# Both products of each MLP as one level of Strassen's scheme, with h kept in memory as seven summed operands

## The chip, the cores and the metric

One core of one Trainium2 chip. The metric is the device time of one execution in microseconds, median over runs. Engines: TensorE (PE, its weight loads shown apart as PEld), VectorE (DVE), ScalarE (ACT), GpSimd (POOL) and SyncE (SP), whose queue issues most DMAs here.

## The reference

A decoder trunk of two layers on x of 1024 tokens by D = 1024, in float32. Layer 0 mixes with an S5 state-space block, layer 1 with stick-breaking attention, whose K and V are projected from the output of layer 0. After each mixer comes an MLP with 4096 hidden features, and each is closed by a layer norm over a scaled residual:

```python
mix = s5_mixer(...)                 # layer 0;  stick_breaking_attention(...) in layer 1
x = layer_norm(DEEPNORM_ALPHA * x + mix, ln_mix_g[layer], ln_mix_b[layer])
h = jnp.square(jax.nn.relu(x @ mlp_w1[layer] + b1))     # 1024 x 4096
ff = h @ mlp_w2[layer] + b2                             # 1024 x 1024
x = layer_norm(DEEPNORM_ALPHA * x + ff, ln_mlp_g[layer], ln_mlp_b[layer])
```

## The kernel before

Every product runs as three matmuls on split operands: a tensor is cast to fp32r by ScalarE (`hi`) and the remainder is formed by VectorE (`lo`), in `split`; a product is hi·hi + hi·lo + lo·hi. Raw weights come by SP in blocks of 128x512 (256 KB, `load_w`).

After its mixer a layer runs `proj_ln`: the output projection by token tile t = 0..7, then per tile the residual, `layer_norm`, and the transposes of y into the activation operand of the MLP (x1T in layer 0, x3T in layer 1). `layer_norm` of one tile goes bn_stats on VectorE, a power on GpSimd, a shift on ScalarE, a scaling on VectorE and the addition of b on GpSimd.

`mlp` has 32 blocks f of 128 hidden features. For each, `up` makes 48 matmuls of 128x128 by 128x512 into two PSUM banks (m0ph, m1ph), `up_act` applies Relu and Square on ScalarE and splits h on VectorE; h stays on chip. `down` takes chunks of two f blocks (the last has four), and for each of the 8 token tiles makes matmuls into m0py or m1py, which VectorE adds into the tile y (m0/m1 are the layers). In the first chunk GpSimd adds the bias b2 to y, in the last every token tile ends in its layer norm and store, or, in layer 0, in the transposes for the K and V projections. `VProject` follows layer 0's MLP. The up of the next chunk is issued between two downs. For the first four f blocks the first token half runs before the transposes of tokens 4 to 7. Pools of weight tiles give the distance by which loads run ahead; instructions within an engine are executed in the order in which they stand.

The lines that matter: L107 `split`'s subtraction, L106 its cast, L154 to L166 the norm, L755 to L759 the down matmuls, L92 to L96 the up matmuls, L764/L766 the additions into y, L768 the bias.

## Time and profile before

| | |
|---|---|
| median of 3 runs | 2547.64 us (2545.24 to 2548.4) |
| profiled execution, its own time | 2546.39 us |
| its span | 2544.7 us |
| TensorE busy | 2431.7 us, 96% |
| VectorE, ScalarE, GpSimd busy | 1503.3 (59%), 869.8 (34%), 537.0 us (21%) |
| DMA, mean | 76 GB/s |

The span is that of the records on the core; the time beside it includes what lies around. The page divides the span in 40 slices of 63.6 us. The MLPs are the two long stretches of slices with digit 9 in TensorE and single digits of DMA.

### The profile page before, as it was taken

The page shows a single profiled execution, that of the slowest core. Times are in us where ns is not written, and L with a number is a line of the kernel's source. Part 1 is how long each engine was busy: PE and PEld are TensorE (multiplying, and loading weights), DVE is VectorE, ACT ScalarE, POOL GpSimd, SP SyncE. Part 2 cuts the span into 40 slices and gives each one's busy share as a digit, 9 for nine tenths or more (in the row PEclk, how much of TensorE's full clock was granted, in tenths as well). Part 3 has the DMA queues.
Part 4 walks back from the last instruction along what each step waited for, and adds up shares of the span by engine and source line. Part 5 has one row for each costly group of instructions (what it writes and reads, how often), then busy time and mean ns, then how long its engine had stood idle before and what let it go on. Part 6 is the DMA issues. An engine that isn't in the chain of part 4 may idle for free.

```text
span 2544.7 us, 31280 instructions
## 1 busy us (share of the span) xinstructions
PE 2431.7 (96%) x11712; PEld 2000.4 (79%) x11712; DVE 1503.3 (59%) x2364; ACT 869.8 (34%) x1707; POOL 537.0 (21%) x620
## 2 busy tenths in 40 slices
...
PEclk9989999999999999999999999998999999999999
...
DMA packets 126248, 194.07 MB, mean 76 GB/s; under 512 B 13968, under 2 KB 56976, under 8 KB 126096
## 3 DMA queue, kind: packets, MB, share of 16 engines
...
## 4 chain that ended last, share of the span: by engine, by line
PE 73%; DVE 8%; issue 3%; POOL 2%; DMA 1%; ACT 1%; POOLq 0%; SPq 0%; DVEq 0%; ACTq 0%
PE m0py L755 5%; PE m0py L757 5%; PE m0py L759 5%; PE m1ph L96 4%; PE m1ph L94 4%; PE m1ph L92 4%; PE m0ph L92 4%; PE m0ph L94 4%; PE m0ph L96 4%; PE m1py L755 4%; PE m1py L757 4%; PE m1py L759 4%; DVE qq L1001 2%; PE po L1028 2%; DVE be L1002 2%
## 5 line engine op out<-in xcount | busy, mean ns | idle before, releaser
L106 ACT CAST w_m<-r_m 128x512 fp32r<-128x512 f32 x256 | 151.6, 620 | 622.8 <-PE m1py L759 257.3
L161 POOL TENSOR_TENSOR rsm<-vem,nhalf 128x1 f32<-128x1 f32 x16 | 9.1, 571 | 1209.5 <-DVE vem L159 1209.5
L107 DVE TENSOR_TENSOR w_m<-r_m,w_m 128x512 fp32r<-128x512 f32 x256 | 195.1, 776 | 110.9 <-ACT w_m L106 110.5
L766 DVE TENSOR_TENSOR y<-y,m1py 128x512 f32<-128x512 f32 x224 | 144.7, 682 | 97.2 <-PE m1py L759 97.2
L766 DVE TENSOR_TENSOR y<-y,m0py 128x512 f32<-128x512 f32 x224 | 144.8, 683 | 96.0 <-PE m0py L759 95.8
L1001 DVE TENSOR_TENSOR_SCAN qq<-qq 128x128 f32<-128x128 f32 (+7 forms) x128 | 174.2, 1363 | 12.0 <-POOL qq L995 11.7
L96 PE MATMUL m1ph<-x3T_h,w_m 128*128 128x512 f32 x512 | 165.1, 394 | 0.0
L94 PE MATMUL m1ph<-x3T_l,w_m 128*128 128x512 f32 x512 | 165.1, 394 | 0.0
L92 PE MATMUL m1ph<-x3T_h,w_m 128*128 128x512 f32 x512 | 164.8, 394 | 0.0
L94 PE MATMUL m0ph<-x1T_l,w_m 128*128 128x512 f32 x512 | 163.9, 391 | 0.0
L96 PE MATMUL m0ph<-x1T_h,w_m 128*128 128x512 f32 x512 | 163.8, 391 | 0.0
L92 PE MATMUL m0ph<-x1T_h,w_m 128*128 128x512 f32 x512 | 163.6, 391 | 0.0
L755 PE MATMUL m0py<-w_m,m0hh 128*128 128x512 f32 x512 | 160.8, 393 | 0.7 <-DVE x1T_l L107 0.5
L755 PE MATMUL m1py<-w_m,m1hh 128*128 128x512 f32 x512 | 160.4, 392 | 0.7 <-DVE x3T_l L107 0.5
L757 PE MATMUL m1py<-w_m,m1hh 128*128 128x512 f32 x512 | 159.8, 392 | 0.0
L759 PE MATMUL m1py<-w_m,m1hl 128*128 128x512 f32 x512 | 159.7, 392 | 0.0
L759 PE MATMUL m0py<-w_m,m0hl 128*128 128x512 f32 x512 | 159.7, 392 | 0.0
L757 PE MATMUL m0py<-w_m,m0hh 128*128 128x512 f32 x512 | 159.6, 392 | 0.0
L729 DVE CAST m1hh<-m1hr 128x512 fp32r<-128x512 f32 x64 | 27.1, 423 | 207.3 <-ACT m1hr L728 207.3
L729 DVE CAST m0hh<-m0hr 128x512 fp32r<-128x512 f32 x64 | 27.1, 423 | 201.9 <-ACT m0hr L728 201.9
L1014 PE MATMUL pt<-ident,be 128*128 128x128 f32 x576 | 90.5, 281 | 33.3 <-DVE wTl L107 23.3
L106 ACT CAST wTh<-pt 128x512 fp32r<-128x512 f32 (+1 forms) x192 | 88.1, 486 | 85.4 <-PE pt L1014 84.8
...
## 6 DMA issues: line engine op xcount, KB each, us to landing
r_m<-in_w SPq DMA_DIRECT2D x256, 256.0 KB, 2.7
v_d<-vt POOLq DMA_DIRECT2D x16, 512.0 KB, 3.5
v<-v_d POOLq DMA_DIRECT2D x16, 512.0 KB, 5.1
khs<-kh POOLq DMA_DIRECT2D x32, 256.0 KB, 3.0
kls<-kl POOLq DMA_DIRECT2D x32, 256.0 KB, 2.9
o_d<-ob SPq DMA_DIRECT2D x128, 64.0 KB, 2.5
ol<-o_d SPq DMA_DIRECT2D x32, 256.0 KB, 3.3
r_win<-in_w_in SPq DMA_DIRECT2D x16, 256.0 KB, 3.4
```

The costliest lines, as they stand in the source:

```text
L92: pe.matmul(ps[h], wh, xa[0][:, k, half(h)], start=(k == 0), stop=False)
L94: pe.matmul(ps[h], wh, xa[1][:, k, half(h)], start=False, stop=False)
L96: pe.matmul(ps[h], wl, xa[0][:, k, half(h)], start=False, stop=(k == KD - 1))
L106: act.copy(hi, src)
L107: dve.tensor_sub(lo, src, hi)
L729: dve.tensor_copy(hh[:, half(h)], r)
L755: pe.matmul(ps[n], hh[:, tok(t)], wh[:, half(n)], start=a0, stop=False)
L757: pe.matmul(ps[n], hh[:, tok(t)], wl[:, half(n)], start=False, stop=False)
L759: pe.matmul(ps[n], hl[:, tok(t)], wh[:, half(n)], start=False, stop=a1)
L766: dve.tensor_add(ys, ys, ps[n])
L1001: dve.tensor_tensor_scan(out=rev, data0=rev, data1=rev, initial=1.0, op0=ALU.mult, op1=ALU.bypass)
L1014: pe.transpose(pt[:, b_], self.be[:, tok(s0 + b_)], ident)
```

## The change

The features, the hidden blocks and the tokens are each taken in halves (2 x 2 blocks), and the eight half products of each matrix product become seven, M1 to M7, of sums of blocks. In `proj_ln` the transposed y of tokens 0 to 3 gives operands B11 and B21, tokens 4 to 7 with `second` and `rest` the other five (B22 and T1 to T4). `mlp_up` goes through 16 pairs p of f blocks with the seven products in the order PROD, 12 matmuls each; the weight operands of four products are sums of w1 blocks made on VectorE. Products are combined into the four blocks of h, Relu and Square are applied, and the sums s1 to s4 and the blocks that the second product needs, seven tensors of 128x512 per pair, are stored to memory (h_d) out of GpSimd's queue. `mlp_down` loads them again: chunks of CH = 4 pairs, per product and pair one unit of 12 matmuls, whose h and w2 operands are prepared three units ahead (`LA`; in up the weight operands are made two products ahead), the sums of w2 on GpSimd. y is stored by `layer_norm` (xm0_d, xm1_d) and loaded again for `mlp_down`. The steps of up run over all 16 pairs, then down begins. The last two M4 units of the last chunk are ordered by token tile, with the norms of tokens 4 to 7 between. The function names of the MLP change from m0/m1 to m0/m1 for up and d0/d1 for down. The core of the diff:

```diff
+    class XOps:
...
+        def first(self, psp, tag, y, t):
+            for kq, (n_, r) in enumerate((("B11", self.r11), ("B21", self.r21))):
+                pt = transpose(psp, tag, y, kq, f"{self.nm}_{t}{kq}")
+                h_, l_ = [v[:, :, tok(t)] for v in self.op[n_]]
+                act.copy(h_, pt)
+                act.copy(r[:, :, tok(t)], pt)
+                dve.tensor_sub(l_, pt, h_)
+        def more(self, tp_, tag, rp):
+            for n_ in ("T1", "T2", "T3", "T4"):
+                self.op[n_] = self.two(tp_, tag, n_)
+            self.r12, self.r22 = [rp.tile([P, 4, HF], F32, name=f"{self.nm}r{i}2") for i in (1, 2)]
+        def second(self, psp, tag, y, t):
+            c = tok(t - 4)
+            pt = transpose(psp, tag, y, 0, f"{self.nm}_{t}0")
+            r = self.r11[:, :, c]
+            dve.tensor_sub(r, r, pt)
+            act.copy(self.r12[:, :, c], pt)
+            pt = transpose(psp, tag, y, 1, f"{self.nm}_{t}1")
+            act.copy(self.r22[:, :, c], pt)
+            h_, l_ = [v[:, :, c] for v in self.op["T1"]]
+            act.copy(h_, r)
+            dve.tensor_sub(l_, r, h_)
+        def rest(self):
+            def both(n_, r):
+                for k2 in range(2):
+                    k = slice(2 * k2, 2 * k2 + 2)
+                    h_, l_ = [v[:, k] for v in self.op[n_]]
+                    act.copy(h_, r[:, k])
+                    dve.tensor_sub(l_, r[:, k], h_)
+            pool.tensor_add(self.r11, self.r11, self.r22)
+            both("B22", self.r22)
+            both("T2", self.r11)
+            dve.tensor_sub(self.r12, self.r22, self.r12)
+            pool.tensor_sub(self.r21, self.r11, self.r21)
+            both("T3", self.r12)
+            both("T4", self.r21)
...
-            for ts in (range(4), range(4, 8)):
+            for ts in (range(4), range(4, 8)) if n == 0 else (range(4), (4, 5), (6, 7)):
...
+    PROD = ("M1", "M5", "M6", "M3", "M7", "M2", "M4")
+    XOP = {"M1": "B11", "M5": "T1", "M6": "T2", "M3": "B22", "M7": "T3", "M2": "B21", "M4": "T4"}
...
+    def mlp_up(l, xo, y_tiles, w1, nm, ypool, tpool, tag, side, uside):
...
+        def prod(p, m, w):
+            ps_, (xh, xl) = bank(p, m), xo.op[XOP[m]]
+            first = m in ("M1", "M5", "M2")
+            for k, (wh, wl) in enumerate(by_k([w])):
+                pe.matmul(ps_, wh, xh[:, k], start=first and k == 0, stop=False, skip_group_check=True)
+                pe.matmul(ps_, wh, xl[:, k], start=False, stop=False, skip_group_check=True)
+                pe.matmul(ps_, wl, xh[:, k], start=False, stop=k == 3, skip_group_check=True)
+        xs = ExitStack()
+        xo.more(tpool, tag, mkpool(xs, f"{nm}r", 1, side=side))
+        for i, (p, m) in enumerate(((0, "M1"), (0, "M2"), (1, "M1"), (1, "M2"))):
+            prod(p, m, w1[i])
+            xo.second(pst, "t", y_tiles[4 + i], 4 + i)
+        xo.rest()
...
+        def operand(p, m):
+            r = lambda i, j: raw[p, i - 1, j - 1]
+            if m in ("M1", "M2", "M4"):
+                src = {"M1": r(1, 1), "M2": r(1, 2), "M4": r(2, 2)}[m]
+            else:
+                src = raws[-1].tile([P, HF], F32, tag="raw", name=f"{nm}s{m}{p}")
+                if m == "M5":
+                    dve.tensor_add(src, r(2, 1), r(2, 2))
+                elif m == "M6":
+                    dve.scalar_tensor_tensor(src, sums[p, "M5"], -1.0, r(1, 1), op0=ALU.mult, op1=ALU.subtract)
+                elif m == "M3":
+                    dve.tensor_sub(src, r(1, 2), sums[p, "M6"])
+                else:
+                    dve.tensor_add(src, r(1, 1), r(2, 1))
+                sums[p, m] = src
+            t = sl[count[0] % len(sl)].tile([P, 2, HF], F32R, tag="w", name=f"w_{nm}1{m}{p}")
+            count[0] += 1
+            split(t[:, 0], t[:, 1], src)
+            return t[:, 0], t[:, 1]
...
+        def after(p, m):
+            if m in ("M1", "M5", "M6"):
+                keep(p, m)
+            elif m == "M3":
+                dve.tensor_add(h_new(p, "A21"), tmp[p, "M6"], bank(p, m))
+                finish(p, "A21", hs[p, "A21"], 1.0, 0)
+            elif m == "M7":
+                dve.tensor_add(h_new(p, "A22"), tmp[p, "M5"], bank(p, m))
+                finish(p, "A22", hs[p, "A22"], -1.0, 1)
+                store(p, "A22", 6)
+                dve.tensor_add(h_new(p, "s1"), hs[p, "A21"], hs[p, "A22"])
+                store(p, "s1", 1)
+            elif m == "M2":
+                dve.tensor_add(h_new(p, "A11"), tmp[p, "M1"], bank(p, m))
+                finish(p, "A11", hs[p, "A11"], 1.0, 0)
+                store(p, "A11", 0)
+            else:
+                h_new(p, "A12")
+                finish(p, "A12", bank(p, m), -1.0, 1)
+                store(p, "A12", 5)
+                h_new(p, "s2")
+                dve.scalar_tensor_tensor(hs[p, "s2"], hs[p, "s1"], -1.0, hs[p, "A11"], op0=ALU.mult, op1=ALU.subtract)
+                store(p, "s2", 2)
+                dve.tensor_add(h_new(p, "s3"), hs[p, "A11"], hs[p, "A21"])
+                store(p, "s3", 4)
+                dve.tensor_sub(h_new(p, "s4"), hs[p, "A12"], hs[p, "s2"])
+                store(p, "s4", 3)
...
+    def mlp_down(ph, l, nm, xd, last, then=None):
...
+        def prep(p, m):
+            r = lambda i, j: raw[p, i - 1, j - 1]
+            if m == "M1":
+                w = r(1, 1)
+            elif m == "M5":
+                w = r(1, 1)
+                pool.tensor_sub(w, w, r(1, 2))
+            elif m == "M6":
+                w = tp_.tile([P, HF], F32, tag="t", name=f"{nm}t{p}")
+                pool.tensor_add(w, r(1, 1), r(2, 2))
+            elif m == "M3":
+                w = r(2, 2)
+            elif m == "M7":
+                w = r(1, 2)
+                pool.tensor_sub(w, r(2, 2), w)
+            elif m == "M2":
+                w = r(2, 1)
+            else:
+                w = r(2, 1)
+                pool.tensor_add(r(1, 1), r(1, 1), r(2, 2))
+                pool.tensor_sub(w, r(1, 1), w)
+            h, wo_ = op_tile(f"H{m}{p}"), op_tile(f"2{m}{p}")
+            split(*h, hraw.pop((p, m)))
+            split(*wo_, w)
+            return h, wo_
...
+        NCH = NP // CH
+        units = [(c, m, p) for c in range(NCH) for m in PROD for p in range(c * CH, (c + 1) * CH)]
+        LA = 3
+        ready = {}
+        for i, part in enumerate(((0, 0), (0, 1), (1, 1), (1, 0))):
+            for p in range(CH):
+                load_raw(p, [part])
+                if i == 0 and p < 2:
+                    load_h(p, "M1")
+            for t in range(4 * i - 4, 4 * i) if i in (1, 2) else ():
+                dma.dma_start(y_tiles[t], xd[tok(t)])
+        gb.append(bcast(cp, A["b2"][l], f"{nm}b2", "gb"))
+        tail = []
+        for i in range(-LA, len(units)):
+            if i + LA + 2 < len(units) and i + LA >= 0:
+                c, m, p = units[i + LA + 2] if i + LA + 2 < len(units) else (0, 0, 0)
+                load_h(p, m)
+            if i + LA < len(units):
+                c, m, p = units[i + LA]
+                ready[p, m] = prep(p, m)
+                if m == "M4" and c + 1 < NCH:
+                    load_raw(p + CH)
+            elif then:
+                then.load(op_tile)
+            if i < 0:
+                continue
+            c, m, p = units[i]
+            q = p % CH
+            fin = c == NCH - 1
+            if q == 0 and m in ("M1", "M5", "M2"):
+                pl = psC if m in ("M5", "M2") else psA
+                banks["A" if m == "M1" else "C"] = [pl.tile([P, HF], F32, tag="p", name=f"{nm}{m}{c}{t}")
+                                                   for t in range(4)]
+            first = q == 0 and m in ("M1", "M5", "M2")
+            lst = q == CH - 1
+            if fin and m == "M4" and q >= CH - 2:
+                tail.append((p, m, ready.pop((p, m)), first, lst))
+                if then and q == CH - 2:
+                    xn = act_tiles(actp, "act", f"{nm}xo")
+                    for t in range(2):
+                        transpose_split(psC, "p", y_tiles[t], t, xn, nm)
+                if q == CH - 1:
+                    for t in range(4):
+                        for p_, m_, ops, f_, l_ in tail:
+                            unit(p_, m_, ops, (t,), f_, l_)
+                        evict(c, m, t)
+                        norm(4 + t)
+                continue
+            unit(p, m, ready.pop((p, m)), range(4), first, lst)
+            if q == CH - 1:
+                for t in range(4):
+                    evict(c, m, t)
+                    if fin and m == "M2":
+                        if not t:
                             gb.append(bcast(cp, A["lnfg"][l], f"{nm}g", "gb"))
+                            gb.append(bcast(cp, A["lnfb"][l], f"{nm}b", "gb2"))
+                        norm(t)
+                if c == 0 and m == "M4":
+                    for y in y_tiles:
+                        pool.tensor_add(y, y, gb[0])
...
```

Three places of the order of instructions. The first is VectorE at the start of the up of layer 0, before the change: w_m01_2 and w_m01_3 are weights of f blocks 2 and 3, y0_7 is the token tile 7, sob and sog the norm's parameters.

```order
L107 TENSOR_TENSOR w_m01_2_3972<-r_m01_20_3973,w_m01_2_3972 128x512
L156 BN_AGGR mvso7_3927<-stso7_3924 128x2
L165 SCALAR_TENSOR_TENSOR y0_6_2757<-y0_6_2757,rsso6_3919,sog_3295 128x1024
L158 TENSOR_SCALAR veso7_3929<-mvso7_3927 128x1
L159 TENSOR_SCALAR veso7_3929<-mvso7_3927 128x1
L107 TENSOR_TENSOR w_m01_2_3972<-r_m01_21_3977,w_m01_2_3972 128x512
L107 TENSOR_TENSOR w_m01_3_3981<-r_m01_30_3982,w_m01_3_3981 128x512
L165 SCALAR_TENSOR_TENSOR y0_7_2758<-y0_7_2758,rsso7_3932,sog_3295 128x512 x2
L107 TENSOR_TENSOR w_m01_3_3981<-r_m01_31_3986,w_m01_3_3981 128x512
L166 TENSOR_TENSOR y0_7_2758<-y0_7_2758,sob_3297 128x512
L107 TENSOR_TENSOR w_m02_0_4286<-r_m02_00_4287,w_m02_0_4286 128x512
```

With the change: ptx1_70 is the transposed token tile 7, x1r, x1r12, x1r22 raw halves, x1B22 and x1T2 to x1T4 operands, m0sM50 the sum and w_m01M50 the weight of the first M5.

```order
L230 TENSOR_TENSOR x1r_3308<-x1r_3308,ptx1_70_4108 128x4x128
L250 TENSOR_TENSOR x1r12_4009<-x1r22_4010,x1r12_4009 128x2048
L236 TENSOR_TENSOR x1T1_4005<-x1r_3308,x1T1_4005 128x4x128
L245 TENSOR_TENSOR x1B22_3307<-x1r22_4010,x1B22_3307 128x1024 x2
L884 TENSOR_TENSOR m0hA110_4202<-m0kM10_4200,m0B0_4039 128x512
L245 TENSOR_TENSOR x1T2_4006<-x1r_3308,x1T2_4006 128x1024 x2
L245 TENSOR_TENSOR x1T3_4007<-x1r12_4009,x1T3_4007 128x1024 x2
L245 TENSOR_TENSOR x1T4_4008<-x1r_3308,x1T4_4008 128x1024 x2
L841 TENSOR_TENSOR m0sM50_4172<-m0r010_4160,m0r011_4162 128x512
L123 TENSOR_TENSOR w_m01M40_4233<-m0r011_4162,w_m01M40_4233 128x512
L843 SCALAR_TENSOR_TENSOR m0sM60_4177<-m0sM50_4172,m0r000_4156 128x512
L123 TENSOR_TENSOR w_m01M50_4174<-m0sM50_4172,w_m01M50_4174 128x512
```

The weight operands that stood between the steps of the last norm now stand behind the splits of the activation operands of `rest`.

The second is SP where up ends and down begins, in layer 0. First, before the change, the place where the first blocks of w2 are loaded (r_m02_..), which follow the w1 blocks of f = 2 and 3:

```order
L116 DMA r_m01_20_3973<-in_w1 128x512
L116 DMA r_m01_21_3977<-in_w1 128x512
L116 DMA r_m01_30_3982<-in_w1 128x512
L116 DMA r_m01_31_3986<-in_w1 128x512
L116 DMA r_m02_00_4287<-in_w2 128x512
L116 DMA r_m02_01_4291<-in_w2 128x512
L116 DMA r_m02_10_4296<-in_w2 128x512
L148 DMA m0b2_3960<-in_b2 128x1024
```

With the change: d0hM10 is h for M1 of pair 0, d0y the token tiles, d0r the raw w2 blocks.

```order
L961 DMA d0hM10_6695<-h_d_80 128x512
L961 DMA d0hM11_6699<-h_d_80 128x512
L961 DMA d0hM12_6739<-h_d_80 128x512
L1027 DMA d0y0_6685<-xm0_d_78 128x1024
L1027 DMA d0y1_6686<-xm0_d_78 128x1024
L1027 DMA d0y2_6687<-xm0_d_78 128x1024
L1027 DMA d0y3_6688<-xm0_d_78 128x1024
L950 DMA d0r000_6693<-in_w2 128x512
L950 DMA d0r100_6697<-in_w2 128x512
L950 DMA d0r200_6701<-in_w2 128x512
```

And twelve rows further on in the same queue:

```order
L1027 DMA d0y6_6691<-xm0_d_78 128x1024
L1027 DMA d0y7_6692<-xm0_d_78 128x1024
L950 DMA d0r010_6729<-in_w2 128x512
L950 DMA d0r110_6731<-in_w2 128x512
L950 DMA d0r210_6733<-in_w2 128x512
L950 DMA d0r310_6735<-in_w2 128x512
L163 DMA d0b2_6737<-in_b2 128x1024
L961 DMA d0hM13_6747<-h_d_80 128x512
L961 DMA d0hM50_6755<-h_d_80 128x512
```

The w2 loads, which ran ahead during up, now come after the loads of four y tiles, and hM13 after those of all eight.

The third is VectorE at the end of layer 0's down. Before, the weights of v projection's second half of k, with the last norms (y0_7) and transposes:

```order
L165 SCALAR_TENSOR_TENSOR y0_6_2757<-y0_6_2757,rsm06_8728,m0g_8390 128x1024
L766 TENSOR_TENSOR y0_7_2758<-y0_7_2758,m0py2871_8749 128x512
L107 TENSOR_TENSOR w_v02_8808<-r_v020_8809,w_v02_8808 128x512
L154 BN_STATS stm07_8776<-y0_7_2758 128x6
L107 TENSOR_TENSOR m0xo_l_3963<-ptm0_50_8794,m0xo_h_3962 128x4x128
L156 BN_AGGR mvm07_8779<-stm07_8776 128x2
```

With the change: w_v03 to w_v07 are weights of v, d0y6 and d0y7 the last token tiles in their norms, d0xo the transposed output.

```order
L123 TENSOR_TENSOR w_v03_9510<-r_v03_9511,w_v03_9510 128x512
L171 BN_AGGR mvd07_9487<-std07_9484 128x2
L180 SCALAR_TENSOR_TENSOR d0y6_6691<-d0y6_6691,rsd06_9471,d0g_9272 128x1024
L173 TENSOR_SCALAR ved07_9489<-mvd07_9487 128x1
L174 TENSOR_SCALAR ved07_9489<-mvd07_9487 128x1
L123 TENSOR_TENSOR w_v04_9515<-r_v04_9516,w_v04_9515 128x512
L123 TENSOR_TENSOR w_v05_9520<-r_v05_9521,w_v05_9520 128x512
L180 SCALAR_TENSOR_TENSOR d0y7_6692<-d0y7_6692,rsd07_9492,d0g_9272 128x512 x2
L123 TENSOR_TENSOR w_v06_9525<-r_v06_9526,w_v06_9525 128x512
L181 TENSOR_TENSOR d0y7_6692<-d0y7_6692,d0b_9274 128x512
L123 TENSOR_TENSOR d0xo_l0_9379<-ptd0_20_9564,d0xo_h0_9377 128x4x128
L123 TENSOR_TENSOR w_v07_9530<-r_v07_9531,w_v07_9530 128x512
```

Five of eight weights of v are now split among and behind the norms of tokens 6 and 7; before it was two of four tiles, each for two k.

## Rows read from the trace of the kernel before

**Rows 1.** The page: busy us (share of the span) and instructions of each engine, the granted TensorE clock in tenths over 40 slices, and the chain that ended last.

```profile
PE 2431.7 (96%) x11712; PEld 2000.4 (79%) x11712; DVE 1503.3 (59%) x2364; ACT 869.8 (34%) x1707; POOL 537.0 (21%) x620
...
PEclk9989999999999999999999999998999999999999
...
PE 73%; DVE 8%; issue 3%; POOL 2%; DMA 1%; ACT 1%; POOLq 0%; SPq 0%; DVEq 0%; ACTq 0%
```

**Rows 2.** Busy time by stretch: start and end, length, busy time (and number) of each engine, granted TensorE clock, DMA share, GB/s. The first two are stretches at the lower level of the clock, then the MLP of layer 0, its inner part, the v projection, the MLP of layer 1, the end.

```profile
276.40:283.00 6.60, 5.24 (x30) 4.63 (x31) 4.32 (x8) 3.52 (x9) 2.69 (x4) 0.50 0.01 2
1720.30:1730.20 9.90, 5.51 (x25) 5.22 (x26) 8.13 (x9) 2.11 (x6) 1.19 (x1) 0.50 0.41 138
475.00:1190.50 715.50, 712.79 (x3145) 583.91 (x3144) 347.39 (x575) 169.45 (x289) 50.21 (x29) 1.00 0.17 54
700.00:1000.00 300.00, 300.00 (x1311) 245.62 (x1310) 130.00 (x216) 62.67 (x109) 0.00 (x0) 1.00 0.16 50
1820.00:2535.30 715.30, 712.60 (x3105) 579.88 (x3103) 340.10 (x561) 160.93 (x272) 50.26 (x29) 1.00 0.16 52
2535.30:2544.70 9.40, 0.18 (x1) 0.00 (x0) 5.04 (x9) 1.33 (x2) 4.55 (x3) 0.72 0.29 112
```

**Rows 3.** TensorE in the up of layer 0: start, duration (matmuls overlap), line, output and operands, number of instructions in the row.

```profile
898.68 0.63 PE L96 MATMUL m0ph<-x1T_h,w_m 128*128 128x512 f32 x2
899.14 0.63 PE L92 MATMUL m0ph<-x1T_h,w_m 128*128 128x512 f32 x2
899.61 0.63 PE L94 MATMUL m0ph<-x1T_l,w_m 128*128 128x512 f32 x2
```

**Rows 4.** The same in the v projection, where three and more matmuls in a row add into one bank, and a token's half of transposes.

```profile
1199.78 0.39 PE L101 MATMUL pv<-w_v,m0xo_h 128*128 128x512 f32 x1
1200.00 0.39 PE L102 MATMUL pv<-w_v,m0xo_h 128*128 128x512 f32 x1
1200.23 0.39 PE L103 MATMUL pv<-w_v,m0xo_l 128*128 128x512 f32 x1
1200.57 1.09 PE L174 MATMUL ptvx<-ident,y 128*128 128x128 f32 x8
```

**Rows 5.** VectorE in the up of layer 0: start, duration, operation.

```profile
903.78 0.68 DVE L107 TENSOR_TENSOR w_m<-r_m,w_m 128x512 fp32r<-128x512 f32 x1
904.39 0.68 DVE L730 TENSOR_TENSOR m0hl<-m0hr,m0hh 128x512 fp32r<-128x512 f32 x1
904.99 0.68 DVE L107 TENSOR_TENSOR w_m<-r_m,w_m 128x512 fp32r<-128x512 f32 x1
```

**Rows 6.** Groups by line and shape, over the whole span: number, busy us and mean ns of one, idle time before and what ended it.

```profile
L107 DVE TENSOR_TENSOR w_m<-r_m,w_m 128x512 fp32r<-128x512 f32 x256 | 195.1, 776 | 110.9 <-ACT w_m L106 110.5
L106 ACT CAST w_m<-r_m 128x512 fp32r<-128x512 f32 x256 | 151.6, 620 | 622.8 <-PE m1py L759 257.3 <-PE m0py L759 257.1 <-DMA r_m<-in_w 94.4
L730 DVE TENSOR_TENSOR m0hl<-m0hr,m0hh 128x512 fp32r<-128x512 f32 x64 | 44.0, 687 | 1.1
L165 DVE SCALAR_TENSOR_TENSOR y<-y,rsso,sog 128x1024 f32<-128x1024 f32 x7 | 9.0, 1285 | 4.8 <-POOL rsso L161 2.7 <-ACT y L164 2.1
L164 ACT ACTIVATE y<-y,vem 128x1024 f32<-128x1024 f32 x14 | 16.1, 1152 | 53.6 <-DVE vem L159 53.6
```

**Rows 7.** GpSimd's addition of b2 and VectorE beside it, in the first down chunk of layer 1: start, duration, operation.

```profile
1874.95 2.52 POOL L768 TENSOR_TENSOR y<-y,m1b 128x1024 f32<-128x1024 f32 x1 [37.17 <-DVE y L764]
1879.90 5.14 POOL L768 TENSOR_TENSOR y<-y,m1b 128x1024 f32<-128x1024 f32 x2 [2.43 <-DVE y L764]
...
1875.13 2.89 DVE L107 TENSOR_TENSOR w_m<-r_m,w_m 128x512 fp32r<-128x512 f32 x1
1880.34 1.27 DVE L764 SCALAR_TENSOR_TENSOR y<-y,m1py 128x512 f32<-128x512 f32 x2
1882.49 0.69 DVE L764 SCALAR_TENSOR_TENSOR y<-y,m1py 128x512 f32<-128x512 f32 x1 [0.88 <-PE m1py L759]
```

**Rows 8.** GpSimd at the end of layer 0's output projection, where the last four norms run one after the other.

```profile
477.25 2.40 POOL L166 TENSOR_TENSOR y<-y,sob 128x1024 f32<-128x1024 f32 x1 [2.02 <-DVE veso L158]
481.55 2.42 POOL L166 TENSOR_TENSOR y<-y,sob 128x1024 f32<-128x1024 f32 x1 [1.40 <-DVE veso L158]
486.32 2.90 POOL L166 TENSOR_TENSOR y<-y,sob 128x1024 f32<-128x1024 f32 x1 [1.40 <-DVE veso L158]
491.05 1.74 POOL L166 TENSOR_TENSOR y<-y,sob 128x512 f32<-128x512 f32 x1 [0.87 <-DVE y L165]
```

**Rows 9.** DMA issues: tensor, queue, number, KB each, median us from issue to landing; and two stretches in which eight loads of 512 KB were under way.

```profile
r_m<-in_w SPq DMA_DIRECT2D x256, 256.0 KB, 2.7
khs<-kh POOLq DMA_DIRECT2D x32, 256.0 KB, 3.0
out<-y SPq DMA_DIRECT2D x7, 512.0 KB, 2.6
out<-y SPq DMA_DIRECT2D x2, 256.0 KB, 2.1
...
300.00:304.00 4.00, 4.00 (x19) 3.22 (x18) 0.69 (x1) 0.63 (x1) 2.47 (x2) 1.00 0.98 377
304.00:308.00 4.00, 4.00 (x18) 3.21 (x18) 0.00 (x0) 0.00 (x0) 0.07 (x1) 1.00 1.03 419
```

**Rows 10.** GpSimd in the last chunk of layer 1's down, one norm per token tile.

```profile
2519.02 2.42 POOL L166 TENSOR_TENSOR y<-y,m1b 128x1024 f32<-128x1024 f32 x1 [2.08 <-DVE y L165]
2524.53 2.40 POOL L166 TENSOR_TENSOR y<-y,m1b 128x1024 f32<-128x1024 f32 x1 [2.08 <-DVE y L165]
2530.05 2.41 POOL L166 TENSOR_TENSOR y<-y,m1b 128x1024 f32<-128x1024 f32 x1 [2.08 <-DVE y L165]
```

378 lines of the change are left out of this document (220 added, 158 removed).

## The prediction

> **What bounds the kernel now.** I read the page's busy table and chain first [rows 1]: TensorE (PE) is busy 96% of the span and carries 73% of the chain of waits, so time comes off only where TensorE does less. The table of stretches [rows 2] places this. Each MLP is about 715.5 us long (475 to 1190.5 and 1820 to 2535.3) and PE is busy 712.8 and 712.6 of it; in 700 to 1000 it is busy 300.00 of 300 at a granted clock of 1.00. Two gaps in it cost under 3 us per layer. After the last matmul there are 9.4 us of tail. So MLP time is matmuls times cadence. The cadence: 1311 matmuls in 300 us are 0.2288 us each, and in the timeline [rows 3] pairs start 0.46 to 0.47 us apart, 0.23 each. I use 0.2285. Consecutive matmuls into one PSUM bank, which is how the new products accumulate, start 0.22 to 0.23 apart in the v projection [rows 4], so that arrangement costs nothing.
>
> **What is removed.** Before, an MLP has 2 x 32 x 48 = 3072 matmuls of 128x128 by 128x512. After, each product has 7 x 16 x 12 = 1344, so 2688. Two layers lose 2 x 384 = 768, and 768 x 0.2285 = **175.5 us**. The transposes stay. The Trainium skill (*TensorE: Matmul & The Clock Gate*, section "Back-to-back issue gap") gives about 131 ns as the sustained spacing of matmuls of this width, each with its own weight load; by that the saving would be 100.6 us, and the rows' cadence disagrees with it.
>
> **What is added in the steady state, and its cover.** The window is one pair of f blocks, 7 x 12 matmuls, 84 x 0.2285 = 19.2 us. VectorE (DVE) operations of 128x512 back to back start 0.60 to 0.61 us apart [rows 5]; ScalarE (ACT) casts average 0.62 [rows 6].
> Up: 4 operand sums, 7 weight splits, 3 combinations and 4 h sums are 18 DVE operations, 18 x 0.605 = 10.9 us; ACT has 7 casts, 3 copies out of PSUM and 8 Relu or Square, 18 x 0.65 = 11.7. Both fit under 19.2, so TensorE still sets the pace: cost nothing. POOL issues the 7 stores per pair and has nothing else in up; 256 KB out of its queue landed 3.0 us after issue [rows 9]. If the cover were gone, each missing microsecond would come 32 times.
> Down: 14 splits and 7 evictions are 21 DVE operations, 12.7 us; ACT has 14 casts; GpSimd (POOL) 5 weight sums. A POOL add of 128x1024 takes 2.40 [rows 8], so 1.25 at half the size with its issue: 6.25. These exclude each other with DVE splits: a split that averages 0.776 [rows 6] and starts 0.18 us after a POOL add took 2.89, until the add had ended, while DVE operations with one input in PSUM ran at their normal pace during another POOL add [rows 7]. With everything in turn, 12.7 + 6.25 = 18.95 of 19.2. That just fits. In the first chunk of each layer POOL also has 8 adds y + b2 of 2.4 us, 19.2 in all, which do not fit beside it; most is taken up by operands made three units ahead. I take 5 us per layer (bounds 0 and 19), **10**.
> h through memory: 7 x 256 KB x 16 out and back are 59 MB per MLP, on 50 GB/s now [rows 2]; over 614 us that is about 95 GB/s more, against 377 to 419 GB/s with the engines full [rows 9]. Hidden.
>
> **What the seams lose.** Four places where TensorE had cover before.
> (a) Start of each up. TensorE gets four products with weights ready and four pairs of transposes, 4 x 2.74 + 4 x 1.09 = 15.3 us. Then it needs the M5 weight, and DVE has that behind everything that `rest()` emits. In turn after the last transpose: the last r11 and T1 columns 1.3; r22 - r12 (128x2048, twice the 1.28 of L165, 2.5) ; POOL's first 128x2048 add, twice 2.40, 4.8; B22 2.5; hA11 0.7; first cast of T2 1.15 (as L164, [rows 6]); T2 2.5; T3 2.5; POOL's second 4.8; cast 1.15; T4 2.5; four 128x512 operations up to the M5 split 2.4. Sum 28.8. If POOL's 9.6 and the two casts were all hidden, 16.9. The exclusion in [rows 7] speaks for the upper value, and I take it. After idling, PE shows a granted clock of 0.50 for 6.6 and 9.9 us [rows 2]; I add 3 us. 31.8 x 2 = **63.6**.
> (b) Up to down. The w2 blocks that ran ahead before now wait in SP's queue behind hM10 to hM12 and four loads of y (512 KB each), some of them waiting for the last M4 to give up its memory: 2.1 MB at 400 GB/s are 5.2 us, landing of r000 2.7, cast and split 1.3: first unit about 8.5 to 9 late. The fourth unit needs hM13, which stands behind 12 raw blocks, y4 to y7, four more blocks and b2, 9.2 MB or 23 us at 400 GB/s, less what had started before the end of up; three units of cover after the first bring us to about 17; I take 4.5 to 5 late. 13.5 x 2 = **27** (bounds 17, if hM13 is in time, and 40).
> (c) End of d0. Eight norms start at M2's last eviction. POOL's adds at the end of the output projection start 4.3 to 4.8 us apart [rows 8], so the splits of w_v03 to w_v07, behind norms 4 to 7 in DVE, are finished some 7.25 x 4.7 = 34 us after M2. TensorE has the last M4 units, 11 us, and two tokens' transposes, 2.2, in that time. Idle 34 - 13 = 21; **20** (bounds 10 and 25).
> (d) End of d1. Before, each norm lies behind 24 matmuls (POOL adds 5.5 us apart, [rows 10]), and only 9.4 us remain behind PE. After, eight norms behind 11 us: 8 x 4.7 = 37.6 plus landing 2.1 to 2.6 [rows 9] is about 40 after M2, or 29.7 after the ideal end of PE, 20.3 more than now: **20.3** (bounds 10, if half of the norms overlap, and 25).
> Sum: -175.5 + 10 + 63.6 + 27 + 20 + 20.3 = -34.6. The profiled execution took 2546.4 (span 2544.7 and 1.7 around it), so **2512 us**; the median of the runs, 2547.6, is 1.2 higher, inside their spread.
>
> **Rivals.** *A, the forecast*, 2490 to 2540 by its own terms: chance 0.52.
> *B, seams at their lower bounds*: POOL's adds and the norms' steps pipeline instead of queueing. 2 x 16.9 + 17 + 10 + 10 = 71, no loss in the first chunks, and -175.5 + 71 = -104.5: **2442**. For it: the norms of DVE, ACT and POOL work on different tokens at once. Against: the norm rows [rows 8] are already such an overlapped run and stay at 4.7. Chance 0.17.
> *C, slower*: in down, DVE with POOL becomes the bound. If DVE operations cost their mean durations of 0.687 instead of the 0.605 spacing, 21 x 0.687 + 6.25 = 20.7 us per pair against 19.2: 1.5 x 32 = 48 more, **2560**. It decides from a spacing of (19.2 - 6.25)/21 = 0.617 us on, 2% above what [rows 5] show. For it: [rows 7], and a POOL add that has to wait for DVE's gaps. Against: the 7 evictions read PSUM and need not exclude POOL. The Trainium skill (*SBUF — State Buffer*, section "SBUF: two separate sides") calls the pair of ports an exclusive lock, held for a whole instruction; the split of 2.89 us agrees. Chance 0.18.
> *D, no change*: the seams each cost some 8 us more than worked out, through DMA landings in (b) and half clock in (c), about 2545. Chance 0.13; it splits over the three signs.
> From no change a measurement of this kernel can tell about 0.2%, 5 us. Faster: A, B and a third of D, 0.73. Same 0.07. Slower: C and a little of D, 0.20. The range 2450 to 2560 leaves out half of B and half of C.
>
> **What would show it.** Steady stretches of up with PE at 0.2285 us per matmul and DVE near 60%; down with DVE and POOL together near 95% and PE still full (C: PE idle released by DVE splits in every pair). Before the first M5 matmul of each layer an idle stretch of 25 to 32 us released by DVE's split of w_m01M50 and w_m11M50; 8 to 9 us before the first down matmul, released by a DMA, and about 5 before the unit of hM13. v projection's first matmul waiting for w_v07. A tail of some 30 us after the last matmul. Wrong if the start of up idles under 15 us (B), or if down runs above 20 us per pair (C).

## The result, and the profile after

The changed kernel takes **2565.1 us** (median of four runs, 2564.5 to 2570.2) against 2548.0 for the kernel before beside it: a ratio of 1.0073 (95% interval 1.0055 to 1.0090). It is slower by 17 us where 35 us faster was forecast. The profiled execution took 2564.5, span 2562.8.

The page of the changed kernel answers to [rows 1]: busy time, clock and chain.

```profile
PE 2297.2 (90%) x10944; PEld 1876.4 (73%) x10944; DVE 1869.9 (73%) x2638; ACT 1215.8 (47%) x2259; POOL 925.5 (36%) x1008
...
PEclk9988999889999899998999999999989999799998
...
PE 51%; issue 13%; DVE 13%; POOL 5%; DMA 4%; ACT 2%; SPq 0%; POOLq 0%; DVEq 0%; ACTq 0%
```

TensorE executes exactly the 768 matmuls fewer. Yet it is busy only 134.5 us less, not 175, and it idles 152.6 us more (2562.8 - 2297.2 against 2544.7 - 2431.7). The chain says the same: PE's share falls from 73% to 51%. The missing 41 us of busy time are the same work done more slowly: some 34 of them at a lower clock (TensorE was busy at the granted level 0.50 for 121.9 us, before for 53.4, and half of that time is lost), the rest mostly from a slightly longer spacing of the matmuls in up. The windows show where, with the columns of [rows 2]:

```profile
476.30:497.30 21.00, 16.66 (x80) 13.22 (x78) 14.54 (x23) 7.87 (x13) 5.62 (x4) 0.92 0.29 100
497.30:523.20 25.90, 0.00 (x1) 0.00 (x0) 22.28 (x15) 12.36 (x16) 11.48 (x3) 0.60 0.21 69
523.20:530.00 6.80, 6.78 (x16) 4.90 (x17) 5.97 (x10) 3.40 (x6) 0.00 (x0) 0.52 0.59 203
...
826.40:840.30 13.90, 0.07 (x2) 0.02 (x1) 2.87 (x6) 3.15 (x6) 2.52 (x5) 0.63 0.99 352
840.30:850.60 10.30, 10.25 (x36) 7.67 (x36) 2.46 (x4) 1.59 (x3) 6.63 (x6) 0.83 0.99 351
850.60:859.70 9.10, 0.00 (x0) 0.00 (x0) 0.50 (x1) 1.15 (x3) 3.32 (x3) 0.68 1.04 406
930.90:937.60 6.70, 0.01 (x1) 0.04 (x1) 6.70 (x7) 1.14 (x2) 6.21 (x4) 0.87 0.30 78
966.00:1019.00 53.00, 53.00 (x234) 43.48 (x233) 41.79 (x61) 22.63 (x40) 14.49 (x11) 1.00 0.58 182
...
1172.60:1211.90 39.30, 25.26 (x95) 18.71 (x95) 35.33 (x55) 14.43 (x21) 24.21 (x14) 0.79 0.36 127
...
2540.60:2562.70 22.10, 0.00 (x0) 0.00 (x0) 16.63 (x30) 4.62 (x5) 14.56 (x9) 0.57 0.32 130
```

Between the seams TensorE is full (966 to 1019, 53.00 of 53 with DVE at 41.8). At each seam it stands still, and the stretch behind begins at the lower of its two clock levels: 16 instructions in 6.8 us at a granted 0.52 behind the first gap. The waits of TensorE name what ended each gap (us in total, times, longest):

```profile
PE m0C L807 <- ACT w_m01M L122: 25.9, 1, 25.9
...
PE m1C L807 <- ACT w_m11M L122: 23.1, 1, 23.1
PE d0M L996 <- ACT w_d02M L122: 23.0, 2, 13.8
PE d1M L996 <- ACT w_d12M L122: 22.1, 2, 11.3
...
PE d0M L996 <- DVE d0y L1010: 6.7, 1, 6.7
PE d1M L996 <- DVE d1y L1010: 6.7, 1, 6.7
...
PE d0M L996 <- DVE d0y L1012: 3.5, 2, 1.7
```

The first two rows are the start of up, the next two the first and the fourth unit of down in each layer. L1010 and L1012 are evictions of the banks that M4 filled, for which M1 of the next chunk waits (the chunks are the four groups of four pairs): L1010 at the start of the second chunk, L1012 at the two later chunk boundaries.

By sections, each counted from the end of the output projection ahead of it: layer 0's MLP with the v projection is 819.4 us long (806.2 before), layer 1's MLP to the end 726.2 (724.6), everything else 3.4 longer.

### The profile page after: what moved, and what is told of

Its sections match the earlier page's. It is cut to its first block, busy times and chain, and to the rows that moved or that the text cites. A ratio compares the mean times of both kernels' runs of the same rounds, so it can differ in the third digit from the quotient of the medians.

```text
span 2562.8 us, 32294 instructions
## 1 busy us (share of the span) xinstructions
PE 2297.2 (90%) x10944; PEld 1876.4 (73%) x10944; DVE 1869.9 (73%) x2638; ACT 1215.8 (47%) x2259; POOL 925.5 (36%) x1008
## 3 DMA queue, kind: packets, MB, share of 16 engines
q1 hardware_dynamic: 123440, 227.73, 28.8%
## 4 chain that ended last, share of the span: by engine, by line
PE 51%; issue 13%; DVE 13%; POOL 5%; DMA 4%; ACT 2%; SPq 0%; POOLq 0%; DVEq 0%; ACTq 0%
PE d0M L997 3%; PE d0M L996 3%; PE d0M L998 3%; PE d1M L996 3%; PE d1M L997 3%; PE d1M L998 3%; PE m1A L807 2%; PE m1A L809 2%; PE m1A L808 2%; POOL h_d L869 2%; DVE qq L1289 2%; DVE be L1290 2%; PE po L1316 1%; PE pt L1302 1%; PE m1C L807 1%
## 5 line engine op out<-in xcount | busy, mean ns | idle before, releaser
L996 PE MATMUL d0M<-w_d02M,w_d0HM 128*128 128x512 f32 x448 | 177.3, 396 | 33.2 <-ACT w_d02M L122 23.0
L996 PE MATMUL d1M<-w_d12M,w_d1HM 128*128 128x512 f32 x448 | 177.3, 397 | 32.2 <-ACT w_d12M L122 22.1
L997 PE MATMUL d1M<-w_d12M,w_d1HM 128*128 128x512 f32 x448 | 179.3, 400 | 7.2 <-DVE w_d12M L123 7.1
L997 PE MATMUL d0M<-w_d02M,w_d0HM 128*128 128x512 f32 x448 | 177.8, 397 | 2.4 <-DVE w_d02M L123 2.3
L998 PE MATMUL d1M<-w_d12M,w_d1HM 128*128 128x512 f32 x448 | 178.5, 398 | 0.0
L998 PE MATMUL d0M<-w_d02M,w_d0HM 128*128 128x512 f32 x448 | 177.5, 397 | 0.0
L122 ACT CAST w_d0HM<-d0hM 128x512 fp32r<-128x512 f32 x112 | 69.8, 623 | 193.3 <-PE d0M L998 158.8
L123 DVE TENSOR_TENSOR w_d0HM<-d0hM,w_d0HM 128x512 fp32r<-128x512 f32 x112 | 101.1, 902 | 68.4 <-ACT w_d0HM L122 68.4
L123 DVE TENSOR_TENSOR w_d1HM<-d1hM,w_d1HM 128x512 fp32r<-128x512 f32 x112 | 102.8, 918 | 63.0 <-ACT w_d1HM L122 62.9
L996 PEld LDWEIGHTS d0M<-w_d02M,w_d0HM 128*128 128x128 f32 x448 | 85.7, 191 | 54.0 <-ACT w_d02M L122 28.1
L996 PEld LDWEIGHTS d1M<-w_d12M,w_d1HM 128*128 128x128 f32 x448 | 85.7, 191 | 53.0 <-ACT w_d12M L122 27.2
L1302 PE MATMUL pt<-ident,be 128*128 128x128 f32 x576 | 90.9, 282 | 34.1 <-DVE wTl L123 25.2
L1302 PEld LDWEIGHTS pt<-ident,be 128*128 128x128 f32 x576 | 70.0, 143 | 60.1 <-issue 15.6
L123 DVE TENSOR_TENSOR wTl<-pt,wTh 128x512 fp32r<-128x512 f32 (+1 forms) x192 | 99.6, 545 | 10.9 <-ACT wTh L122 10.9
L997 PEld LDWEIGHTS d1M<-w_d12M,w_d1HM 128*128 128x128 f32 x448 | 86.1, 192 | 29.0 <-DVE w_d12M L123 9.8
L1290 DVE TENSOR_TENSOR be<-be,qq 128x127 f32<-128x127 f32 (+7 forms) x128 | 99.3, 776 | 6.6
```

Source lines behind the costliest of these rows:

```text
L122: act.copy(hi, src)
L123: dve.tensor_sub(lo, src, hi)
L996: pe.matmul(ps_, hh[:, tok(t)], wh, start=first, stop=False, skip_group_check=True)
L997: pe.matmul(ps_, hh[:, tok(t)], wl, start=False, stop=False, skip_group_check=True)
L998: pe.matmul(ps_, hl[:, tok(t)], wh, start=False, stop=last, skip_group_check=True)
L1290: dve.tensor_mul(be[:, 0:ns - 1], be[:, 0:ns - 1], qq[:, 1:ns])
```

## The experiments

The theory was that each gap has a cause of its own (queue order, two engines that exclude each other, one engine's backlog) and can be taken away alone. The standing rival was that the gaps have a common cause (memory traffic, the lower clock), so that they move when one is closed. Where one time is given, it belongs to the profiled execution; the changed kernel's is 2564.5, span 2562.8. Parts of the kernel that no edit touches differ by a few us between executions (the first matmul of layer 0's up starts anywhere from 472.2 to 478.9), so I also give the gain **in the MLPs**: from the first matmul into an m0 tile to the last of the v projection, and from the first into an m1 tile to the end, 818.7 and 726.3 us in the changed kernel. Each single edit has one execution, and this measure has noise too: where no edit touches it, layer 0's up alone is 347.8 to 350.6 us long. Gains of 2 us or less say nothing.

**The order of loads at the start of down.** What came ahead of the gaps, in the changed kernel: SP's issues (start, length, number), and ACT's first casts with what ended its idle time.

```profile
827.58 1.49 SPq L1027 DMA_DIRECT2D d0y<-xm_d  x1
829.18 14.02 SPq L950 DMA_DIRECT2D d0r<-in_w  x12
843.77 2.88 SPq L1027 DMA_DIRECT2D d0y<-xm_d  x4
847.00 2.33 SPq L950 DMA_DIRECT2D d0r<-in_w  x4
850.23 0.33 SPq L163 DMA_DIRECT2D d0b<-in_b  x1
851.46 2.84 SPq L961 DMA_DIRECT2D d0hM<-h_d  x3
...
839.61 0.62 ACT L122 CAST w_d02M<-d0r 128x512 fp32r<-128x512 f32 x1 [7.78 <-DMA d0r<-in_w]
...
858.55 0.62 ACT L122 CAST w_d0HM<-d0hM 128x512 fp32r<-128x512 f32 x1 [16.60 <-DMA d0hM<-h_d]
```

The first raw block went out at 829.18 and was not cast before 839.61, while the windows show the DMA engines full at 352 GB/s; hM13 went out only at 851.46. The edit asks for y0 to y3 with the first unit and for the rest of y and b2 with the fourth, in the source behind the first raw blocks and h:

```
-            for t in range(4 * i - 4, 4 * i) if i in (1, 2) else ():
-                dma.dma_start(y_tiles[t], xd[tok(t)])
-        gb.append(bcast(cp, A["b2"][l], ...))
+            if i in (0, 3):          # inside the loop over units
+                for t in range(4 * i // 3, 4 * i // 3 + 4):
+                    dma.dma_start(y_tiles[t], xd[tok(t)])
+                if i: gb.append(bcast(cp, A["b2"][l], ...))
```

> Only the place of the loads of y and b2 at the start of down is changed: y0 to y3 are asked for with the first unit, y4 to y7 and b2 with the fourth. Theory Q (queue order): the first w2 block and hM13 are late because 2 to 9 MB stand ahead of them in SP's queue; the idle time before the first down matmul goes from 13.8 and 11.4 to about 11 and 10 us, the idle time before the fourth unit (9.2 and 10.7 us) goes, and the half clock behind it; span about 24 us shorter than the changed kernel's 2562.8, near 2539. Rival M (memory): the w2 blocks wait until the last h stores have read the memory that they are to fill; both idle times stay, span 2555 or more.

Measured 2541.4, span 2539.7; 20.3 less in the MLPs. This edit alone brings the MLPs below those of the kernel before (1524.7 us against 1531.2). In the whole time one run cannot tell the two apart: the kernel before took 2546.8 beside it and 2540.3 to 2550.0 in all its runs.

```profile
PE d0M L996 <- ACT w_d02M L122: 15.0, 1, 15.0
PE d1M L996 <- ACT w_d12M L122: 10.8, 1, 10.8
```

One wait per layer where there were two: the fourth unit's is gone, so it was hM13's place in SP's queue (it now goes out at 827.30). The first gap stays near what it was. That doesn't clear the order of loads there, since the queue didn't come out as the source has it: in layer 0 three loads of y, in layer 1 two, still go out ahead of the first raw block.

```profile
824.47 0.60 SPq L1033 DMA_DIRECT2D d0y<-xm_d  x1
...
832.51 0.44 SPq L1033 DMA_DIRECT2D d0y<-xm_d  x1
833.00 11.93 SPq L950 DMA_DIRECT2D d0r<-in_w  x16
```

**The additions of b2.** The changed kernel adds b2 to all eight y tiles behind M4 of chunk 0. POOL and DVE there, in layer 0:

```profile
919.84 10.84 POOL L1076 TENSOR_TENSOR d0y<-d0y,d0b 128x1024 f32<-128x1024 f32 x4 [6.63 <-DVE d0y L1012]
...
922.72 2.88 DVE L123 TENSOR_TENSOR w_d02M<-d0r,w_d02M 128x512 fp32r<-128x512 f32 x1
925.53 2.89 DVE L123 TENSOR_TENSOR w_d0HM<-d0hM,w_d0HM 128x512 fp32r<-128x512 f32 x1
928.34 2.88 DVE L123 TENSOR_TENSOR w_d02M<-d0r,w_d02M 128x512 fp32r<-128x512 f32 x1
931.15 0.68 DVE L123 TENSOR_TENSOR w_d0HM<-d0hM,w_d0HM 128x512 fp32r<-128x512 f32 x1
```

Splits that take 0.68 alone take 2.88 each, one per POOL add, and the evictions queue behind them. The edit puts one addition behind each product of later chunks:

```
-                if c == 0 and m == "M4":
-                    for y in y_tiles: pool.tensor_add(y, y, gb[0])
+                g = c * len(PROD) + PROD.index(m) - len(PROD)
+                if 0 <= g < 8: pool.tensor_add(y_tiles[g], y_tiles[g], gb[0])
```

> Only the eight additions y + b2 are moved: instead of four and four in a row at the end of the first chunk, one behind each product of the second chunk and of the first of the third. Theory P (the burst of additions holds the VectorE splits back): idle time and half clock of 12.2 and 11.8 us around the start of the second chunk fall to 2 or less each, span near 2541. Rival: the operands are late there for another reason (the VectorE queue or the h loads); span 2557 or more. If one addition per 11 us is already too much, the second chunk gets slower instead: over 2563.

Measured 2543.8, span 2542.1; 18.6 less in the MLPs. The wait for d0y L1010 falls from 6.7 to 1.7 in both layers, the smaller gaps behind it are gone. The theory holds: the eight additions in a burst cost some 9 us per layer, which the forecast had bounded by 0 and 19 and taken as 5.

**The start of up, in two ways.** First the operands of M5, M6 and M3 of the first two pairs ahead of `rest()` (with the raw blocks' memory taken first, so that they can load early):

```
-        xo.rest()                       # was ahead of every operand
+        load_raw(0); load_raw(1)
+        for p in range(2):
+            for m in ("M5", "M6", "M3"): ready[p, m] = operand(p, m)
+            prod(p, "M5", ready.pop((p, "M5"))); keep(p, "M5")
+        xo.rest()
```

> Only the start of up is changed: the raw w1 blocks get the memory of the y tiles instead of part of r12 and r22, the weight operands of M5, M6 and M3 of pairs 0 and 1 are made before rest(), and the two pairs' products run interleaved in the order in which their activation operands come. Theory W (TensorE idles for one weight operand whose VectorE steps and loads stand behind rest()): idle time of 25.9 and 23.1 us before the first M5 falls to about 11 each and little appears later, span about 26 us shorter, near 2537. Rival C (the chain of rest() itself is the bound: B22, T2, T3, T4 come too late for M3, M6, M7, M4): the idle time moves behind M5 and the gain is under 8 us, span 2555 or more.

Measured 2546.9, span 2545.2: in between. In the MLPs 15.0 less, of which 13.5 in layer 0. Up itself (its first matmul to its last) got only 7.9 and 4.6 shorter in the two layers. The gap of 25.9 becomes four of 10.78, 4.19, 0.67 and 0.67, 16.3 in all. The rest is the start of down, where the edit moved the pools' memory: its two waits went from 23.0 to 15.9 in layer 0, which adds to the gain, and from 22.1 to 25.2 in layer 1, which eats most of it. DVE and POOL in layer 0 say why more was not won:

```profile
498.74 1.22 DVE L245 TENSOR_TENSOR x1B<-x1r,x1B 128x1024 fp32r<-128x1024 f32 x1
499.87 4.99 DVE L839 TENSOR_TENSOR m0sM<-m0r,m0r 128x512 f32<-128x512 f32 x1
504.79 5.54 DVE L245 TENSOR_TENSOR x1B<-x1r,x1B 128x1024 fp32r<-128x1024 f32 x1
...
498.96 5.35 POOL L247 TENSOR_TENSOR x1r<-x1r,x1r 128x2048 f32<-128x2048 f32 x1 [12.47 <-DVE x1T L236]
504.39 4.85 POOL L251 TENSOR_TENSOR x1r<-x1r 128x2048 f32<-128x2048 f32 x1
```

The M5 sum, 0.69 elsewhere, takes 4.99 and ends half a us behind POOL's operation; a 1.22 us split takes 5.54 beside the next. The Trainium skill (*SBUF — State Buffer*, section "SBUF: two separate sides") says that a VectorE operation with two inputs in SBUF is blocked for the whole of a GpSimd instruction that reads SBUF and started first; these rows agree. So the second way moves the two POOL operations of `rest()` to DVE and changes nothing else:

```
-            pool.tensor_add(self.r11, self.r11, self.r22)
+            dve.tensor_add(self.r11, self.r11, self.r22)
-            pool.tensor_sub(self.r21, self.r11, self.r21)
+            dve.tensor_sub(self.r21, self.r11, self.r21)
```

> Only the two 128x2048 operations of rest() are moved from GpSimd, where they took 5.35 and 5.38 us, to VectorE, where the third one of that size took 2.29. Theory X (GpSimd's additions and VectorE's splits exclude each other, so that they stand in one line): each start of up gets 2 x (5.4 - 2.3) = 6 us shorter, span near 2550. Rival: GpSimd's two operations lie beside VectorE's work; VectorE then has 4.6 us more per layer, span 2563 to 2572.

Measured 2553.3, span 2551.6; 8.4 less in the MLPs, all of it in up (5.6 and 2.9). The gaps fall to 21.6 and 20.6.

```profile
500.17 2.28 DVE L247 TENSOR_TENSOR x1r<-x1r,x1r 128x2048 f32<-128x2048 f32 x1
```

On DVE each of the two takes 2.28 where POOL took 5.35 and 5.38 and stopped DVE meanwhile: an engine that gets help here is slower than one that works alone. Together with the first edit (last experiment) the gap is 6.5.

**The boundaries of chunks.** M4 adds to the banks that M1 of the chunk opened, and M1 of the next chunk wants them again.

```
-                pl = psC if m in ("M5", "M2") else psA
+                pl = psC if (m in ("M5", "M2")) != (c == 1) else psA
```

> One cause by itself: the two groups of four PSUM banks change places in the second of the three chunks of down, so that M1 of a chunk no longer takes the banks that M4 of the chunk before has just filled. Theory (the 1.73 to 1.74 us gaps at the chunk boundaries are M1 waiting for the evictions of M4's four blocks, and nothing else comes due in their place): the two gaps of each layer go, four in all, 7 to 8 us, time about 2557. Rival (the operands of the next chunk are late there too, and the gap only changes its name): under 2 us gained, 2562 to 2565.

Measured 2559.2, span 2557.5; 5.7 less in the MLPs. The expectation miscounted: there are four chunks, and a swap in the second serves the boundaries on either side of it, not the last. So one of the two 1.7 us waits per layer went (`d0M <- DVE d0y L1012` from 3.5 to 1.7), the other stayed, and the 6.7 us wait at the second chunk became three of 1.7 to 2.6 for splits. The theory holds for the boundaries that the edit reaches.

**The end of each layer.** With the products of the last chunk in the order M2, M1, M5, M6, M3, M7, M4 the first half of tokens is complete earlier:

```
+                 for m in (("M2",) + PROD[:5] + ("M4",) if c == NCH - 1 else PROD)
-                    if fin and m == "M2":      # norms of tokens 0 to 3
+                    if fin and m == "M3":
```

> Only the order of products in the last chunk of each down is changed: M2, M1, M5, M6, M3, M7, M4 instead of M1, M5, M6, M3, M7, M2, M4, so that tokens 0 to 3 are finished after M3 and their norms have M7 and M4, 22 us, as cover instead of 11. Theory N (eight norms of 4.7 us in a row are the tail): the 22.1 us behind the last matmul fall by about 10, v projection starts about 9 us earlier, M7 to M4 costs 1.7 each for the shared bank, span near 2547. Rival: the tail is set by the norms of tokens 4 to 7 alone, after the last M4, and stays; span 2558 or more.

It gained nothing: 2562.5, span 2560.8, and 1.9 more in the MLPs. The tail behind the last matmul falls from 22.1 to 18.4, but the four norms, now ahead of M4 in DVE, hold its operands back: gaps of 4.6 and 6.1 in layer 1, 7.7 in layer 0. Then the same order with each of these norms behind another unit (the cut is from the second of the two kernels that follow):

```
+        SPR = {("M7", 0): 0, ("M7", 1): 1, ("M7", 3): 2, ("M4", 0): 3}
+            if fin and (m, q) in SPR: norm(SPR[m, q])
```

> As e6_last_order (2560.8 span), but the norms of tokens 0 to 3 follow the first, second, fourth and fifth unit behind M3 instead of standing in a row behind it. Theory B (in e6 the gain in the tail was paid back, since the norms in a row held back the splits of M4's operands, 10.7 us of idle time before M4 in layer 1): that idle time falls under 3 us, the tail of 18 us stays, span near 2549. Rival: the norms are merely later and the tail grows; 2557 or more.

This kernel left out the additions of b2, so its 2538.2 contains what their burst had cost: of the 26.0 that it gained in the MLPs the spread of b2 gave 18.6 alone, and some 7 are left for the order and the norms. With b2 kept:

> The order of products in the last chunk is M2, M1, M5, M6, M3, M7, M4 (so that the last product adds to one half only), and the norms of tokens 0 to 3 are put one behind each of four later units instead of behind the eviction of one product. Nothing else changes. Theory (the norms' long DVE and POOL operations held back the operand splits of M4 when all four stood together, and spread they do not): against the changed kernel 4 to 12 us less, 2553 to 2561, with no gap over 2 us at M4's first units. Rival (the end of the kernel is the norm of the last token behind the last eviction, whatever comes ahead of it): under 3 us gained, 2562 to 2565.

Measured 2554.5, span 2552.8, but only 5.1 less in the MLPs; 3.5 of it is the last chunk boundary, which no longer waits since M2 comes first there. A 6.1 us gap (`d1M <- DVE ved L174`, a norm) still stands at the end of layer 1. The theory's size is right and its reason is not: in layer 1 down with the end got no shorter (368.3 us against 368.4), though the tail behind the last matmul fell from 22.2 to 19.9.

**The first gap of down.** Two queues, with y on POOL's, M1's h loads early and five h buffers instead of three:

```
-                dma.dma_start(y_tiles[t], xd[tok(t)])
+                    pool.dma_start(y_tiles[t], xd[tok(t)])
-        hr = mkpool(ph, f"{nm}hr", 3)
+        hr = mkpool(ph, f"{nm}hr", 5)
```

> As e1_load_order (2539.7 span), but y is loaded from GpSimd's queue, all four h blocks of M1 are asked for beside the first four w2 blocks, and h has five buffers instead of three, so that nothing in SP's queue stands before w2 but h. Theory Q (order in SP's queue): the idle time before the first down matmul, 15.0 and 10.8 us in e1, falls to about 8, span near 2530. Rival (the 16 DMA engines are full with whatever is issued first, from either queue): as e1, 2537 to 2542.

It lost: 2569.8, span 2568.1. The larger pool shifts the raw blocks of w2 onto memory from which the last h is stored, so in layer 0 the first goes out at 834.9 and the gap grows to 18.7; in layer 1 it goes out at 2193.4, behind six loads of h, and the gap is 21.8. That suggested memory, not order, as what holds the first block back. In the changed kernel SP's own waits in 820 to 865 have this row, three waits for stores of h to land:

```profile
SPq L950 <- DMA h_d<-m0hs: 7.9, 3, 4.5
```

These waits stand ahead of the second raw block and of later ones, though. The first went out at 829.18, before any of them, and TensorE is full as soon as it has the first unit (10.25 of 10.30 us from 840.3), so in layer 0 of the changed kernel they cost nothing. The next edit gives w2's blocks other memory, on top of the first experiment's order of loads:

```
+        wr2 = mkpool(wst if then else ph, f"{nm}wr", CH + 1, side="right" if then else None)
+        tp_ = mkpool(wst if then else ph, f"{nm}tp", 2, side="right" if then else None)
         yp = mkpool(ph, f"{nm}y", 8)    # wr2 and tp_ were opened last, on the other side
```

> The load order of the earlier run (tokens 0 to 3 of y with the first unit, the rest and b2 with the fourth), and beside it the raw blocks of w2 get memory that nothing at the end of up uses: in layer 1 the first blocks then wait for an early product of up alone; in layer 0 they still share memory with tiles that the last stores of h read. Theory S (the first gap of down, 15 us in layer 0 and 11 in layer 1, is a load of w2 that cannot be issued before its memory is free, then its landing and the splits): layer 1's gap falls from 11 to 0 to 5 us, layer 0's stays within 4 us of 15, time 2530 to 2538. Rival (the first gap is what the stores of h and the loads that read them take, about 8 us behind the last product of up, whatever w2 does): both gaps stay, time about 2541.

Measured 2544.6, span 2542.9: no gain over the order of loads alone (gaps 14.2 and 9.2). In layer 0 that was expected. In layer 1 the theory fails as put. The first raw blocks do go out at 2160.9, 14 us before up ends, but ACT then idles for something else:

```profile
2182.86 0.62 ACT L122 CAST w_d1HM<-d1hM 128x512 fp32r<-128x512 f32 x1 [6.65 <-DMA d1hM<-h_d]
```

The two h operands stand behind raw blocks that wait in SP's queue for `PE m1A L809`, up's last product, to free memory (11.6 us). So it takes both, free memory and a place in the queue ahead of every load that waits; the last experiment has both in layer 1.

**Everything that gave something, together.** First with the two-queue version, and without the additions of b2:

> e9_two_queues, e2_bias_spread, e5_operands_first, e8_rest_dve and e7_norms_spread together, and in the second chunk of each down the two groups of PSUM banks swapped, so that M1 does not wait for M4's eviction. If the causes are separate (theory S), the gains add: about 33 + 21 + 18 + 8 + 14 + 4 us from 2562.8, near 2465, faster than the kernel before by some 3%. Rival: they overlap (the same DVE time gained twice), and it stays above 2500.

Measured 2495.5 (ratio 0.9802, 0.9782 to 0.9822), between the theory's 2465 and the rival's "above 2500"; the first gaps of down still 11.7 and 18.3. Then with the loads of the first experiment, w2's other memory, and b2 kept:

> Everything that gave something, together, and the whole computation kept: load order of y, b2's additions spread one per product, bank groups swapped in the second chunk, the operands of M5, M6 and M3 of the first two pairs ahead of the rest of x's combinations, their two 128x2048 operations on DVE, norms of tokens 0 to 3 spread in the last chunk, and w2's raw blocks in memory that the end of up does not use. Theory (the single gains add, since each was a gap of its own place): against 2564.5, less 21 for the loads, 19 for b2, 7 for the banks, 30 to 45 for the start of up, 2 to 5 for the end, and 10 to 25 for w2's place: 2440 to 2475, likeliest 2465, a ratio to the kernel before near .968. Rival (the loads of w2, y and h contend however they are ordered, and the start of down stays at 15 us a layer or more): 2485 to 2500. In both cases faster than the kernel before; slower than 2540 would mean that the gaps have one common cause which moves with the edits.

Measured **2482.4** (five runs, 2478.4 to 2484.2), ratio to the kernel before **0.9740** (0.9727 to 0.9754), which is 66 us faster than before and 83 faster than the changed kernel. That is 7 above the theory's range and 3 below that of the rival named there. In the MLPs 80.2 less; the single gains (20.3, 18.6, 5.7, 15.0, 8.4, 5.1) add to 73.1. By place they agree less well. Up got 29.7 shorter, where the two edits to it had given 12.5 and 8.5. Down and what follows it got 39.7 shorter, where the single edits had given some 50 there. The first gaps of down lost 10.9, mostly in layer 1, 2.3 where it was 11.3, since h now goes out at 2113.6 ahead of the raw blocks at 2118.3:

```profile
PE d0M L1007 <- ACT w_d02M L122: 12.0, 1, 12.0
...
PE d1M L1008 <- DVE w_d12M L123: 7.2, 8, 1.8
PE m1C L807 <- ACT w_m11M L122: 6.5, 1, 6.5
PE m0C L807 <- ACT w_m01M L122: 6.5, 1, 6.5
PE d1M L1007 <- DVE ved L174: 6.1, 1, 6.1
...
PE d1M L1007 <- ACT w_d12M L122: 3.0, 2, 2.3
```

Each gap could be closed, and the time is far from the 2540 that a common cause would have kept, so that rival falls. That the sums agree is in part luck: in down some 11 us of the gains overlap, and I did not trace where. Layer 0's 12 us stay: there a load of y, ahead of w2 in SP's queue, waits 9.8 us for one of up's last products. Freeing that was not tried.

## Why the prediction was wrong

The lost time, both layers together, beside the forecast's terms (the measured values are estimates from the windows and waits above; they count idle time and what the lower clock behind the gap cost):

| step | forecast | measured |
|---|---|---|
| 768 matmuls fewer | -175.5 | -175.7 |
| (a) start of up | 63.6 | 64.6 |
| (b) up to down | 27 | 55.2 |
| POOL's additions of b2 | 10 | 24.0 |
| (c) end of d0 | 20 | 21.6 |
| (d) end of d1 | 20.3 | 19.5 |
| boundaries of later chunks | not seen | 7.8 |
| spacing in up | 0 | 8.1 |
| sum | -34.6 | +25.1 |

The two MLPs grew by 14.7. The 10.4 between that and the sum is what the kernel before lost itself: 5.4 of it are gaps in [rows 2], and most of the rest is its spacing in layer 1, where 2519 matmuls took 580 us, 0.2303 each, against 0.2288 in layer 0: 4.5 us over 3072.

**Right.** The saving. That the steady state is hidden: down is PE-bound at 53.00 of 53, so rival C, which held the chance for slower, is false although the time came out on its side. POOL's 128x512 sums are longer than the 1.25 of the sum (1.28 to 1.75), but DVE, their waits included, is busy 41.8 of 53. (a) in sum to within 1 us, by the mechanism named (idle 30.3 in 476.3 to 530 and about 4 of lower clock), but with some luck in it: the gap before M5 was 25.9 and 23.1 where the chain had 28.8, in layer 0 its last 2.8 were a wait of DVE for the raw block `m0r`, and 4.3 and 4.6 of idle came earlier, where the transposes wait for ScalarE's copies, which the forecast had at nothing. (c) and (d) in sum, not in parts, and that is luck. (c): 39.3 us with 14.0 of idle, where 20 were forecast; the mean clock of 0.79, which had no term there, makes up the rest. (d): the tail was 22.1, not "some 30 us"; 4.7 of idle ahead of the last matmuls and about 2 of lower clock, which had no term, bring it to the value, less the 9.4 of [rows 2].

**Wrong, by size: (b).** The forecast had "first unit about 8.5 to 9 late", from 2.1 MB ahead of r000 and "landing of r000 2.7"; it was 13.8 and 11.4. The step that failed is what r000 shared the DMA engines with. In the 13.9 us of layer 0's gap they moved 352 GB/s, that is some 4.9 MB and not 2.1, among them the last five stores of h, issued from GpSimd's queue from 826.2 to 830.0. At the forecast's 400 GB/s these are 12.2 us where it had 5.2. This is read from the trace; no run took the stores away.

```profile
826.21 0.54 POOL L869 DMA_DIRECT2D h_d<-m0hA  x1 [1.48 <-ACT m0hA L862]
826.93 1.15 POOL L869 DMA_DIRECT2D h_d<-m0hs  x2 [0.18 <-issue]
829.19 0.54 POOL L869 DMA_DIRECT2D h_d<-m0hA  x1 [1.11 <-ACT m0hA L862]
829.98 0.54 POOL L869 DMA_DIRECT2D h_d<-m0hs  x1 [0.26 <-DVE m0hs L896]
```

And it gave the landing its unloaded time from [rows 9], but r000 was cast 10.4 us after its issue, in a stretch with the engines full. The fourth unit was 9.2 and 10.7 late, not "4.5 to 5". The remaining 4 to 6 per layer are the lower clock behind each gap, which the forecast charged at (a) alone. The upper bound of 40 was passed, so the bound was wrong too: it counted the loads' bytes, and neither the stores nor the lower clock.

**Wrong, by choice: the first chunk.** The bounds, 0 and 19 per layer, held the value (12 with the bank wait of 1.7 and the lower clock; the edit that spread the additions won 9.3 per layer). I took 5, on the argument that operands made three units ahead absorb it. But the splits that stand still are those operands.

**Not in the sum.** The bank group that M4 leaves to the next M1 (four boundaries of 1.7, and part of the gap at the second chunk). And the spacing in up, 0.2311 and 0.2318 in the two layers (1281 and 1277 matmuls in 296 us at a granted clock of 1.00), where the forecast had 0.2285; its cause was not tried.

The terms that were seen were all nearly right in sum or too small. Each was a chain of durations with nothing else in its way, and rival D (no change, "some 8 us more" per seam) named this with a chance of 0.13 but stopped short of the side on which it ended.
